# One more weight buffer, the last norm's weights loaded last, a rearranged last norm, and half of the first gather as bf16 products

## The chip, the cores and the metric

One NeuronCore of a Trainium2 chip runs the whole program in one launch. It has TensorE (PE in the rows; its weight loads are PEld), VectorE (DVE), ScalarE (ACT), GpSimd (POOL) and a queue engine, SyncE (SP), all in order within themselves and tied by semaphores, and 16 DMA engines. The metric is the device time of one execution in microseconds (us), the median of several. Lower is better.

## The reference

A decoder block on 256 tokens of width 1024 with 16 meta tokens ahead: a mixer, then a mixture of 16 experts, then a last norm. The change touches what follows the mixer.

```python
h = h + concat(y_ssd, y_sc) @ w_out          # 272 x 2048 @ 2048 x 1024
u2 = rmsnorm(h, norm_ffn)
# hier_moe(u2): best of 4 groups, in it the best 2 of 4 experts, weights by softmax
for e in range(16):
    out += combine[:, e:e+1] * ((silu(t @ w_gate[e]) * (t @ w_up[e])) @ w_down[e])   # 1024 x 512, 512 x 1024
h = h + out
return rmsnorm(h, norm_final)[:, 16:]
```

The experts' weights are 96 MB in float32 (16 experts, three matrices of 2 MB), and each is read once.

## The kernel before

**Stages.** First the mixer (about 223 us), then the routing (to about 240 us): tokens stand on partitions in two halves b = 0, 1 of 128, `hh[:, b]` holds their normalised rows, `scores` and `places` mark each token's two experts, `ranks` gives each token its place `rk` in its experts' queues. Then the experts, 64 slots each, in seven units: `UNITS = 6 * [2] + [4]`. The six experts of the first three units are fixed; `sort_experts` sorts the other ten by load and writes `order` (the numbers that the later loads' addresses come from) and `mosti` (whether an expert has more than 64 tokens; a branch at the very end uses it).

**A unit.** `pick` makes a 0/1 matrix P (token to slot), a gather multiplies hh by it on PE, `rows` scales it into X, then `gu` (gate, then up), ACT's Silu and DVE's product `hb`, its transposes `hbp`, then `yd` (down), `weighed` splits the result into two float32r parts, `scatter` adds them into the PSUM tiles `acc[b][n]` (half b of the tokens, half n of the 1024 columns) during the next unit's gate. The next unit's gather stands between a unit's up and down. Unit 0's gather (`gather`, L903) multiplies float32; later ones (`gather3`, L1115) multiply three bf16 parts of hh, whose sum is hh. These parts are made once, after unit 0's X: for each half two ACT copies and two DVE subtractions, and at the end two ACT copies more (L1101 to L1108).

**The stream of weights.** SP issues all weight loads in the order of use, 1 MB each, into `RING + RING2` = 22 + 3 slots, one of which holds hh then. A load waits on SP until its slot's last reader is done: `used(n)` stands after every second quarter of a product. So 24 MB lie ready before unit 0, and its first gate products free the next slots. The last unit's second halves of `w_down` come in pieces (512 KB, then twice 256 KB for each of four experts). `fin`, the last norm's weights repeated on 128 partitions, is a tile of its own of 4 KB a partition, loaded during the mixer (L774).

**The end.** The last unit's down product comes in column thirds of 512, 256 and 256 (`THIRDS`). `squares_of` (ACT) sums squares of acc; `last_norm` takes the root, and per half of tokens DVE multiplies both column halves by root and `fin`, and ACT's queue issues the four stores.

**Order.** It is written out by hand (`manual_schedule`): each engine runs its instructions in the order of the code.

Of the kernel before, what the change touches and what calls it, by code (L numbers as in the profile page):

```python
# [17 lines left out]
KT = 8  # L18
NE, CAP = 16, 64
EPS = 1e-6  # L20
RING, RING2 = 22, 3
# [18 lines left out]
def body(ctx, tc, x, meta_tokens, norm_mix, w_in, ssd_conv_w, ssd_conv_b, dt_bias, A_log, D_skip,  # L40
# [90 lines left out]
    comb = cp.tile([128, 2, NX], F32, name="comb")  # L131
    count16 = cp.tile([128, NE], F32, name="count16")
    chain = cp.tile([128, NE - FIXED, NE - FIXED], F32, name="chain")
    place = cp.tile([128, NE - FIXED], F32, name="place")
    order = cp.tile([128, NE - FIXED], I32, name="order")

    fin = cp.tile([128, D], F32, name="fin")
    lg = cp.tile([128, 2, 20], F32, name="lg")
    cnt = cp.tile([128, 2, 5, 4], F32, name="cnt")
# [600 lines left out]
    for i, (name, j, c, t0) in enumerate(units):  # L740
# [108 lines left out]
    def ranks(b):  # L849

        p = rp[:, 64 + 16 * b:80 + 16 * b]
        T.matmul(p, sup, mem[:, b], start=True, stop=(b == 0))
        if b:
            T.matmul(p, onesb, mem[:, 0], start=False, stop=True)
        V.scalar_tensor_tensor(rk[:, b, 0:NE], mem[:, b], -1024.0, p, op0=OP.mult, op1=OP.add)
# [20 lines left out]
    def sort_experts(counts):  # L876
        m, key = NE - FIXED, place
        t = small("srt", 2 * m * m)
# [21 lines left out]
    def gather(b, q, p, i0=0, i1=4):  # L900

        for i in range(i0, i1):
            T.matmul(p[:, i], hh[:, b].rearrange("p (m k) -> p k m", k=KT)[:, 4 * q + i],  # L903
                     P[:, b], start=(b == 0 and i == 0), stop=(b == 1),
                     skip_group_check=True)
# [57 lines left out]
    P = bp.tile([128, 2, 128], F32, name="P")  # L963
# [33 lines left out]
    def weights(tm):  # L997
# [20 lines left out]
        in_order(comb[:, :, NE:NX], comb[:, :, FIXED:NE], sorting)  # L1018
# [7 lines left out]
    sorting = wk.tile([128, 2 * (NE - FIXED) ** 2], F32, name="sorting", tag="Yl")  # L1026
# [4 lines left out]
    def back(P, cm):  # L1031
# [8 lines left out]
        PT = wk.tile([128, S], F32R, name="PT", tag="PT")  # L1040
# [44 lines left out]
    h3 = wk.tile([128, 2, D], BF, name="h3")  # L1085
    tm = wk.tile([128, S], F32, name="tm", tag="PT")
    X = wk.tile([128, KT, 128], F32, name="X")
    for q in range(2):
        rows(X, xp[q], q)
    weights(tm)  # L1090
    ws0 = wk.tile([128, 1], F32, name="ws", tag="ws")
    P = wk.tile([128, 2, 128], BF, name="P", bufs=2)
    for b in range(2):
        pick(P, 0, b)


    hb0, hb1 = (hh[:, b].bitcast(BF).rearrange("p (j d) -> p j d", j=2) for b in range(2))
    hparts = [[h3[:, 0], hb0[:, 0]], [h3[:, 1], hb0[:, 1]], [hb1[:, 0], hb1[:, 1]]]
    rem = [wk.tile([128, 512], F32R, name="rem", tag=t).bitcast(BF) for t in ("Yh", "Yl")]
    for b in range(2):  # L1100
        A.activation(hparts[0][b], hh[:, b], AF.Copy)  # L1101
        if b == 0:
            A.activation(ws0, eps, AF.Silu)
        V.tensor_tensor(hh[:, b], hh[:, b], hparts[0][b], op=OP.subtract)
        A.activation(hparts[1][b], hh[:, b], AF.Copy)
        V.tensor_tensor(rem[b], hh[:, b], hparts[1][b], op=OP.subtract)
    for b in range(2):
        A.activation(hparts[2][b], rem[b], AF.Copy)  # L1108
# [20 lines left out]
    def over():  # L1129
# [46 lines left out]
    rv = nc.values_load(mosti[0:1], min_val=0, max_val=2 * S)  # L1176
    chosen += nc.values_load_multi_w_load_instructions(
        order[0:1], engines=[mybir.EngineType.SP], min_val=FIXED, max_val=NE - 1,
# [135 lines left out]
```

## Time and profile before

| | us |
|---|---|
| median of 3 runs | 444.64 (443.95 to 445.56) |
| the profiled execution | 445.38 |
| its span, first to last instruction | 443.4 |

| engine | busy us | share of the span |
|---|---|---|
| PE | 423.8 | 96% |
| PEld | 295.0 | 67% |
| DVE | 220.3 | 50% |
| ACT | 159.0 | 36% |
| POOL | 89.1 | 20% |
| DMA, queue of SP | 138.22 MB | 82.5% of 16 engines |

PE's 96% counts pipelined products whose ends are modelled, so it says that PE is seldom idle, not that it is at its peak. The rows are read by stage: where the chain of waits passes, and what the DMA engines do meanwhile.

### The profile page before, as it was taken

To read this page: it belongs to the slowest core of one execution; us is meant where nothing else is said; L and a number is where in the kernel's file an instruction comes from. 1 tells how busy PE (TensorE), PEld (TensorE's weight loads), DVE (VectorE), ACT (ScalarE), POOL (GpSimd) and SP (SyncE) were. 2 spreads that over 40 slices of the span, in tenths; PEclk is the share of its full clock that TensorE was granted. 3 is DMA by queue.
4 is the path that set the end of the run, shared out by engine and by line. 5 is a ranking of instruction groups with operands and counts; after the bars stand their busy time and mean duration, and the time that the engine had idled before them with its cause. 6 is when DMAs were issued, how large, how long until landed. Compare 5 with 4: busy or idle time off the path is not lost.

```text
span 443.4 us, 7446 instructions
## 1 busy us (share of the span) xinstructions
PE 423.8 (96%) x2923; PEld 295.0 (67%) x2923; DVE 220.3 (50%) x465; ACT 159.0 (36%) x247; POOL 89.1 (20%) x113
## 2 busy tenths in 40 slices
PE   8899999899999899999999999999999999999982
PEld 5799999799998899888877363533535335353241
DVE  7769888758795768695557521110212102121013
ACT  6766346645757344744472401010010100101121
POOL 2345334854668154000000000000000000000000
PEclk9999999999999999999999989999999999999997
DMA  8997977066699566599692999999999999999952
GB/s 232 342 312 250 348 250 266 32 191 188 194 360 413 182 209 233 199 407 419 199 362 102 370 400 375 425 418 424 419 421 421 422 418 420 421 418 422 412 224 98
DMA packets 48892, 139.85 MB, mean 315 GB/s; under 512 B 6342, under 2 KB 32342, under 8 KB 36822
## 3 DMA queue, kind: packets, MB, share of 16 engines
q1 hardware_dynamic: 47990, 138.22, 82.5%
q10 hardware_dynamic: 864, 1.12, 0.7%
q8 instruction: 25, 0.41, 0.4%
q14 instruction: 13, 0.11, 0.1%
HBM read 138.26 MB, written 1.06 MB: 314 GB/s over the span
## 4 chain that ended last, share of the span: by engine, by line
PE 64%; DVE 7%; ACT 3%; issue 2%; POOL 1%; DVEq 0%; ACTq 0%
PE gu L1050 22%; PE yd L1050 11%; PE acc L347 10%; PE xp L1115 4%; PE p_c L339 3%; PE acc L1071 3%; PE p_h L339 3%; PE p_b L339 3%; ACT f L310 1%; PE hbp L1057 1%; DVE h L619 1%; PE xp L903 1%; DVE f L326 1%; POOL f L324 1%; DVE h L548 1%
## 5 line engine op out<-in xcount | busy, mean ns | idle before, releaser
L1050 PE MATMUL gu<-w,X 128*64 128x512 f32 (+1 forms) x512 | 100.0, 595 | 0.4 <-DVE X L1082 0.4
L324 POOL TENSOR_TENSOR f<-w,f 128x256 fp32r<-128x256 f32 x96 | 82.6, 892 | 87.5 <-ACT f L310 77.7
L310 ACT ACTIVATE f<-w 128x1024 fp32r<-128x1024 f32 x64 | 67.1, 1054 | 35.9 <-POOL f L324 12.6
L1050 PEld LDWEIGHTS gu<-w,X 128*64 128x64 f32 (+1 forms) x512 | 31.3, 130 | 61.2 <-issue 59.5
L326 DVE TENSOR_TENSOR f<-w,f 128x1024 fp32r<-128x1024 f32 x40 | 50.6, 1264 | 17.4 <-ACT f L310 17.4
L1050 PE MATMUL yd<-w,hd 128*64 128x512 f32 (+2 forms) x288 | 50.9, 548 | 0.5 <-DVE hd L1060 0.5
L347 PE MATMUL acc<-f,h 128*128 128x512 f32 x192 | 44.8, 391 | 0.0
L1202 DVE TENSOR_TENSOR hb<-hb,gu 128x512 f32<-128x512 f32 x7 | 4.8, 688 | 74.0 <-PE gu L1050 71.9
L347 PEld LDWEIGHTS acc<-f,h 128*128 128x128 f32 x192 | 35.5, 188 | 7.7 <-issue 0.4
L1065 ACT ACTIVATE Yh<-yd,ws 128x512 fp32r<-128x512 f32 x13 | 8.9, 688 | 79.2 <-PE yd L1050 62.5
L1050 PEld LDWEIGHTS yd<-w,hd 128*64 128x64 f32 (+1 forms) x288 | 16.7, 128 | 29.3 <-issue 25.5
L1066 DVE SCALAR_TENSOR_TENSOR Yl<-yd,ws,Yh 128x512 fp32r<-128x512 f32 x12 | 9.0, 751 | 53.6 <-PE yd L1050 38.5
L1115 PE MATMUL xp<-P,hh 128*128 128x128 bf16 x192 | 20.1, 232 | 0.0
L1115 PEld LDWEIGHTS <-hh 128*128 128x128 bf16 x192 | 18.8, 149 | 1.6 <-issue 1.6
L1115 PE MATMUL xp<-P,h 128*128 128x128 bf16 x96 | 17.7, 235 | 1.6 <-ACT hb L1196 1.6
L339 PE MATMUL p_z<-uh,f 128*128 128x256 f32 x128 | 17.3, 285 | 1.9 <-POOL f L324 1.9
L339 PE MATMUL p_c<-uh,f 128*128 128x258 f32 x128 | 16.8, 283 | 1.3 <-DVE h L607 1.3
L339 PE MATMUL p_xs<-uh,f 128*128 128x272 f32 x128 | 18.0, 292 | 0.0
L1196 ACT ACTIVATE hb<-gu 128x512 f32<-128x512 f32 x7 | 4.2, 594 | 37.0 <-PE gu L1050 37.0
L339 PEld LDWEIGHTS p_z<-uh,f 128*128 128x128 f32 x128 | 15.6, 188 | 2.4 <-POOL f L324 2.3
L339 PE MATMUL p_b<-uh,f 128*128 128x256 f32 x128 | 16.6, 281 | 0.7 <-DVE h L607 0.7
L1042 ACT ACTIVATE PT<-ptp 128x256 fp32r<-128x256 f32 x7 | 2.7, 385 | 39.7 <-PE ptp L1038 39.7
(331 smaller groups left out, 648.5 us busy)
## 6 DMA issues: line engine op xcount, KB each, us to landing
w<-in_expert_w_gate SPq DMA_DIRECT2D x32, 1024.0 KB, 11.7
w<-in_expert_w_up SPq DMA_DIRECT2D x32, 1024.0 KB, 14.5
w<-in_expert_w_down SPq DMA_DIRECT2D x28, 1024.0 KB, 13.6
w<-in_w_in SPq DMA_DIRECT2D x23, 1024.0 KB, 7.2
w<-in_w_out SPq DMA_DIRECT2D x8, 1024.0 KB, 9.4
abc<-adr SPq DMA_DIRECT2D x2, 1024.0 KB
w<-in_expert_w_down SPq DMA_DIRECT2D x4, 512.0 KB
w<-in_expert_w_down SPq DMA_DIRECT2D x8, 256.0 KB, 10.5
```

The source lines that it names most:

```text
L310: A.activation(h, src, AF.Copy)
L324: G.tensor_tensor(l[:, k:k + 2], src[:, k:k + 2], h[:, k:k + 2].bitcast(F32), op=OP.subtract)
L326: V.tensor_tensor(l, src, h.bitcast(F32), op=OP.subtract)
L339: T.matmul(p, st_[:, k, :], mv[:, k, t0:], start=(k == 0 and st_ is terms[0][0] and mv is uh), stop=(k == KT - 1 and mv is ul))
L347: T.matmul(acc[b][n], st_[:, 128 * b:128 * (b + 1)], mv[:, 512 * n:512 * (n + 1)], start=False, stop=False, skip_group_check=True)
L548: V.tensor_tensor(yt(4 * hf, 4), yt(4 * hf, 4), v["zs"][:, 4 * hf:4 * hf + 4], op=OP.mult)
L1050: T.matmul(o[c * s:c * s + c], X[:, 128 * k + c * s:128 * k + c * s + c], ws_, start=first_, stop=last_, tile_position=(0, c * s))
L1065: A.activation(Yh, y, AF.Copy, scale=ws)
L1066: V.scalar_tensor_tensor(Yl, y, ws, Yh.bitcast(F32), op0=OP.mult, op1=OP.subtract)
L1071: T.matmul(acc[b][n], PT[:, 128 * b:128 * (b + 1)], part, start=False, stop=stop and part is Y[-1], skip_group_check=True)
L1115: T.matmul(p[:, i], hparts[j][b].rearrange("p (m k) -> p k m", k=KT)[:, 4 * q + i], P[:, b], start=(j == b == 0), stop=(j == 2 and b == 1))
L1202: V.tensor_mul(hb, hb, g)
```

## The change

- **Buffer.** `fin` leaves its early tile. The small routing tiles (`chain`, `place`, `count16`, `comb`, `lg`, `cnt`) become views of one tile `early`, which later is `PT`. The room makes a 26th slot, `RING3 = 1`, in memory that the routing's work tiles held; it opens, with one load, after the routing.
- **Loads.** `fin` is loaded into a freed slot in the last unit, behind the last piece of weights. SP reads `order` after unit 0's up, and all engines read `mosti` after unit 1's down; before, both came ahead of unit 0's gate.
- **Gather of unit 0.** Half b = 0 stays float32. Half b = 1 is split into its three bf16 parts at once and gathered by 24 bf16 products; half b = 0 is split after X.
- **Sorting.** `sort_experts` runs after X and after that split, ahead of `weights`.
- **Last norm.** acc times `fin` for the first column half goes into `wh` before the root is known; ACT then scales it, DVE does the second column half only; the stores are issued by SP and ACT, two each. The second third's result is split into float32r parts (`Y1`), the last third is `Y2`.

```diff
-RING, RING2 = 22, 3
+RING, RING2, RING3 = 22, 3, 1
@@ in the mixer
             load(RING2, right)
-            nc.sync.dma_start(fin, raw(norm_final, 0, [[0, 128], [1, D]]))
@@ routing
-    gather(0, 0, xp[0])
+    gather(0, 0, xp[0], 0, 3)
     for i in range(4):
         places(1, i)
-    gather(0, 1, xp[1], 0, 1)
     ranks(1)
-    gather(0, 1, xp[1], 1, 4)
-    pick(P, 0, 1)
+    P1 = bp.tile([128, 2, 128], BF, name="P1")
+    A.activation(h3[:, 0], hh[:, 1], AF.Copy)
+    V.tensor_tensor(hh[:, 1], hh[:, 1], h3[:, 0], op=OP.subtract)
+    A.activation(h3[:, 1], hh[:, 1], AF.Copy)
+    V.scalar_tensor_tensor(rk[:, 1, 0:NE], mem[:, 1], -1024.0, rp[:, 80:96], op0=OP.mult, op1=OP.add)
+    pick(P1, 0, 1)
+    rem1 = hh[:, 1].bitcast(BF)[:, 0:D]
+    V.tensor_tensor(rem1, hh[:, 1], h3[:, 1], op=OP.subtract)
+    gather(0, 0, xp[0], 3, 4)
+    gather(0, 1, xp[1])
...
-    sort_experts(rp[:, 96:112])
-    for q in range(2):
-        gather(1, q, xp[q])
+    for js in ((0, 1), (2,)):
+        for k in range(KT):
+            for j in js:
+                T.matmul(xp[k // 4][:, k % 4], (h3[:, 0], h3[:, 1], rem1)[j]..., P1[:, 1], start=False, ...)
     es.close()
+    ring3 = ctx.enter_context(tc.tile_pool(name="ring3", bufs=RING3, side="right"))
+    load(RING3, ring3)
@@ after unit 0's X
+    A.activation(hparts[0][0], hh[:, 0], AF.Copy)
+    V.tensor_tensor(hh[:, 0], hh[:, 0], hparts[0][0], op=OP.subtract)
+    A.activation(rem, hh[:, 0], AF.Copy)
+    V.tensor_tensor(hparts[2][0], hh[:, 0], rem, op=OP.subtract)
+    A.activation(hparts[1][0], rem, AF.Copy)
+    sort_experts(rp[:, 96:112], sorting[:, 0:2 * (NE - FIXED) ** 2])
     weights(tm)
@@ the end
+    def by_weights(b, n):
+        V.tensor_tensor(wh[:, b], acc[b][0], fin[:, 0:512], op=OP.mult)
...
             for b in range(2):
                 squares_of(b, 0)
+                by_weights(b, 0)
+                first_sum(b)
         else:
-            V.tensor_scalar(Y1[:, 256:512], y, ws, None, op0=OP.mult)
+            V.tensor_scalar(Y2, y, ws, None, op0=OP.mult)
```

**VectorE from the last expert mark of the routing to the first steps after X** (mem marks the experts, rk the places, X is unit 0's gathered input). Before, the end of the sort stands ahead of X:

```order
L895 TENSOR_TENSOR place<-place,rp 128x10
L896 TENSOR_REDUCE most<-rp 128x1
L897 TENSOR_REDUCE srt<-place 128x1
L898 TENSOR_TENSOR mosti<-most,srt 128x1
L1082 TENSOR_TENSOR X<-xp,gf 128x512 x2
L1003 TENSOR_REDUCE tm<-lg 128x10
```

and in the changed kernel (h_79 is h3, the bf16 parts):

```order
L855 SCALAR_TENSOR_TENSOR mem<-early 128x16
L984 TENSOR_TENSOR hh<-hh,h_79 128x1024
L986 SCALAR_TENSOR_TENSOR rk<-mem,rp 128x16
L875 TENSOR_TENSOR P_2676<-sl,rk 128x128
L989 TENSOR_TENSOR hh<-hh,h_79 128x1024
L1102 TENSOR_TENSOR X<-xp,gf 128x512 x2
L1114 TENSOR_TENSOR hh<-hh 128x1024
L1116 TENSOR_TENSOR hh<-hh,rem 128x1024
L889 SCALAR_TENSOR_TENSOR early<-rp,early 128x10
```

The sort moved behind X and behind two subtractions of half 0; two subtractions of half 1 moved ahead of X.

**SP at the end of the routing**, before (w_2606 is the 24th of the experts' loads, w_2814 the first into a slot that unit 0 frees):

```order
L113 DMA w_2604<-in_expert_w_down 128x2048
L113 DMA w_2606<-in_expert_w_down 128x2048
L1176 TENSOR_LOAD mosti
L1176 ISA x2
L1177 TENSOR_LOAD order
L113 DMA w_2814<-in_expert_w_gate 128x2048
```

and in the changed kernel (w_2722 is the load into the new slot, w_2790 the first into a freed one):

```order
L113 DMA w_2598<-in_expert_w_down 128x2048
L113 DMA w_2600<-in_expert_w_down 128x2048
L113 DMA w_2722<-in_expert_w_gate 128x2048
L113 DMA w_2790<-in_expert_w_gate 128x2048
L113 DMA w_2792<-in_expert_w_gate 128x2048
```

The reads of mosti and order are gone from here, and one load more stands there; it waits for the last expert counts of the routing (DVE), a routing product (PE) and an ACT copy.

**VectorE at the end**, before:

```order
L1066 SCALAR_TENSOR_TENSOR Y<-yd,ws,Yh 128x512
L1258 TENSOR_SCALAR Y_3920<-yd,ws 128x256
L1266 TENSOR_SCALAR s_2804<-s_2804 128x1 x2
L1278 RECIPROCAL s_2803<-s_2803 128x1
L1281 SCALAR_TENSOR_TENSOR o<-acc_68,s_2803,fin 128x512
L1281 SCALAR_TENSOR_TENSOR o<-acc_69,s_2803,fin 128x512
```

and in the changed kernel (oh holds wh and Y2):

```order
L1086 SCALAR_TENSOR_TENSOR Y_3932<-yd,ws,Y_3932 128x256
L1266 TENSOR_TENSOR oh<-acc_68,fin 128x512
L1269 TENSOR_SCALAR s_2780<-s_2780 128x1
L1266 TENSOR_TENSOR oh<-acc_70,fin 128x512
L1269 TENSOR_SCALAR s_2780<-s_2780 128x1
L1295 TENSOR_SCALAR oh<-yd,ws 128x256
L1310 RECIPROCAL s_2779<-s_2779 128x1
```

Two products with fin now stand ahead of the last third's weighing (L1258 before, L1295 now).

## Rows read from the trace of the kernel before

**Rows 1.** The chain that ended last, unit 0 and part of unit 1: start us, us, what.
```profile
239.80 13.95 PE gu L1050 x64
254.21 1.04 ACT hh L1108
260.84 7.02 PE yd L1050 x32
284.14 0.22 PE ptp L1035 x2
284.52 1.64 PE xp L1115 x24
288.18 7.02 PE yd L1050 x32
```

**Rows 2.** Timeline of routing and unit 0's start: start us, us, engine, line, form.
```profile
228.77 2.34 ACT L813 ACTIVATE hh<-hh,rsh 128x1024 f32<-128x1024 f32 x2
235.34 4.07 PE L903 MATMUL xp<-P,hh 128*128 128x128 f32 x16
235.52 0.17 DVE L880 SCALAR_TENSOR_TENSOR place<-rp,count 128x10 f32<-128x10 f32 x1 [1.07 <-PE rp L980]
238.90 0.16 DVE L898 TENSOR_TENSOR mosti<-most,srt 128x1 int32<-128x1 f32 x1
240.18 0.18 DVE L1003 TENSOR_REDUCE tm<-lg 128x10 f32<-128x40 f32 x1
240.77 1.04 ACT L1101 ACTIVATE h<-hh 128x1024 bf16<-128x1024 f32 x1
244.54 0.49 DVE L865 TENSOR_TENSOR P<-sl,rk 128x128 bf16<-128x128 f32 x2
247.29 1.23 DVE L1106 TENSOR_TENSOR rem<-hh,h 128x1024 bf16<-128x1024 f32 x1 [1.12 <-ACT h L1105]
```

**Rows 3.** Stretches of the stream: us, busy of engines, clock share, DMA share, GB/s.
```profile
235.40:244.30 8.90, 8.51 (x41) 5.77 (x40) 7.78 (x36) 2.67 (x4) 0.00 (x0) 1.00 0.02 6
265.00:267.00 2.00, 2.00 (x12) 0.72 (x10) 0.00 (x0) 0.00 (x0) 0.00 (x0) 1.00 0.76 205
267.00:273.00 6.00, 6.00 (x27) 2.20 (x23) 1.90 (x4) 1.37 (x2) 0.00 (x0) 1.00 0.99 359
273.00:426.00 153.00, 151.55 (x966) 63.75 (x968) 24.79 (x46) 14.26 (x24) 0.00 (x0) 1.00 1.01 419
```

**Rows 4.** The chain in the last unit: its gate and up, thirds 1 and 2, third 3.
```profile
410.46 10.53 PE gu L1050 x96
423.37 6.42 PE yd L1050 x63
430.91 1.86 PE yd L1050 x32
```

**Rows 5.** The page's group of DVE's product of PSUM by SBUF (mean ns of one).
```profile
L1202 DVE TENSOR_TENSOR hb<-hb,gu 128x512 f32<-128x512 f32 x7 | 4.8, 688 | 74.0 <-PE gu L1050 71.9
```

**Rows 6.** Timeline of the end: a sum of squares, the last third's weighing, second and last store.
```profile
431.78 0.20 ACT L1240 ACTIVATION_READ_ACCUMULATOR o<-acc 128x1 f32 x1
432.85 0.48 DVE L1258 TENSOR_SCALAR Y<-yd,ws 128x256 f32<-128x256 f32 x1 [3.73 <-PE yd L1050]
436.81 0.34 ACTq L1282 DMA_DIRECT2D out<-o  x1
438.32 1.15 ACTq L1282 DMA_DIRECT2D out<-o  x1
```

**Rows 7.** Loads by line: KB, us from issue to landing; this one was issued at 184.4.
```profile
fin<-in_norm_final SPq DMA_DIRECT2D x1, 512.0 KB, 12.0
```

**Rows 8.** The tile mosti: its read into PE's registers (ns, start us).
```profile
L1176 PEldq TENSOR_LOAD <-mosti x1: 492/492/492, 239.1 to 239.1; - x1
```

**Rows 9.** Stretches by clock: columns as in rows 3.
```profile
255.80:259.60 3.80, 3.80 (x36) 3.75 (x36) 2.00 (x4) 0.21 (x1) 0.00 (x0) 0.57 1.01 420
421.00:421.83 0.83, 0.00 (x0) 0.00 (x0) 0.69 (x1) 0.00 (x0) 0.00 (x0) 1.00 1.01 395
```

More of the change, by code (lines that the diff above doesn't have):

```diff
@@ L130, in body, with part_of @@
     rk = cp.tile([128, 2, NX], F32, name="rk")
[L131 to L134, printed above, removed]
+    m = NE - FIXED
+    early = cp.tile([128, 2 * NX + 206], F32, name="early", tag="PT")
+    at_ = [0]
+    def part_of(n):
+        at_[0] += n
+        return early[:, at_[0] - n:at_[0]]
+    chain = part_of(m * m).rearrange("p (i j) -> p i j", i=m)
+    place = part_of(m)
+    count16 = part_of(NE)
+    comb = part_of(2 * NX).rearrange("p (b e) -> p b e", b=2)
+    lg = part_of(40).rearrange("p (b i) -> p b i", b=2)
+    cnt = part_of(40).rearrange("p (b s i) -> p b s i", b=2, i=4)
     order = cp.tile([128, NE - FIXED], I32, name="order")
-    fin = cp.tile([128, D], F32, name="fin")
-    lg = cp.tile([128, 2, 20], F32, name="lg")
-    cnt = cp.tile([128, 2, 5, 4], F32, name="cnt")
+    h3 = cp.tile([128, 2, D], BF, name="h3")
     selg = cp.tile([128, 2, 4], F32, name="selg")
@@ L874, in in_order, with sort_experts @@
         V.tensor_reduce(out_, t, axis=AX.X, op=OP.add)
-    def sort_experts(counts):
+    def sort_experts(counts, t):
         m, key = NE - FIXED, place
-        t = small("srt", 2 * m * m)
         c = counts[:, FIXED:NE]
@@ L962, in body @@
     busy(1)
-    P = bp.tile([128, 2, 128], F32, name="P")
+    P = bp.tile([128, 1, 128], F32, name="P")
     pick(P, 0, 0)
@@ L1094, in body @@
         pick(P, 0, b)
[L1097 to L1108, printed above, removed]
     def gather3(P, X, q):
@@ L1174, in over @@
                         scatter(b, n, PTo, Yo)
-    rv = nc.values_load(mosti[0:1], min_val=0, max_val=2 * S)
-    chosen += nc.values_load_multi_w_load_instructions(
-        order[0:1], engines=[mybir.EngineType.SP], min_val=FIXED, max_val=NE - 1,
-        skip_runtime_bounds_check_because="a sum of one of the numbers FIXED to NE - 1 and of zeros")[1]
     left = {}
@@ L1196, in body @@
                 A.activation(hb, g, AF.Silu)
-                if not last:
+                if last:
+                    fin = slot("fin", free.pop(0))[:, 0:D]
+                    nc.sync.dma_start(fin, raw(norm_final, 0, [[0, 128], [1, D]]))
+                else:
                     Pn = wk.tile([128, 2, 128], BF, name="P", bufs=2)
@@ L1206, in body @@
             hd = turned(hb)
+        if u == 0:
+            chosen += nc.values_load_multi_w_load_instructions(
+                order[0:1], engines=[mybir.EngineType.SP], min_val=FIXED, max_val=NE - 1,
+                skip_runtime_bounds_check_because="a sum of one of the numbers FIXED to NE - 1 and of zeros")[1]
         PT, ws = back(P, cparts[:, :, places_of(u)])
@@ L1228, in rest @@
             return weighed(y, ws)
+        if u == 1:
+            rv = nc.values_load(mosti[0:1], min_val=0, max_val=2 * S)
         keep = []
@@ L1232, in body, with first_sum, root @@
         left[0, 3] = [lambda b=b, PT=PT, k=keep: scatter(b, 1, PT, k[0]) for b in range(2)]
+    oh = slot("oh", free.pop(0))
+    wh, Y2 = oh[:, 0:1024].rearrange("p (b d) -> p b d", b=2), oh[:, 1024:1280]
     oo = slot("o", free.pop(0)).rearrange("p (b d) -> p b d", b=2)
-    Y1 = wk.tile([128, 512], F32, name="Y1", tag="X")
+    Y1 = wk.tile([128, 2, 256], F32R, name="Y1", tag="X")
     Y = [wk.tile([128, 512], F32R, name="Yh", tag="Yh"), slot("Y", free.pop(0)).bitcast(F32R)[:, 0:512]]
+    def by_weights(b, n):
+        V.tensor_tensor(wh[:, b], acc[b][0], fin[:, 0:512], op=OP.mult)
+    def first_sum(b):
+        V.tensor_scalar(s4[:, b, 0:1], s4[:, b, 0:1], 1.0 / D, EPS, op0=OP.mult, op1=OP.add)
+    def root(b):
+        A.activation(s3[:, b:b + 1], s4[:, b, 1:2], AF.Sqrt, bias=s4[:, b, 0:1], scale=1.0 / D)
     def squares_of(b, n):
@@ L1278, in last_norm @@
             V.reciprocal(s3[:, b:b + 1], s3[:, b:b + 1])
[L1279 to L1282 removed]
+            V.scalar_tensor_tensor(oo[:, b, 512:1024], acc[b][1], s3[:, b:b + 1], fin[:, 512:1024], op0=OP.mult,
+                                   op1=OP.mult)
+            nc.sync.dma_start(raw(out, b * 128 * D + 512, [[D, 128], [1, 512]]), oo[:, b, 512:1024])
+        for b in range(2):
+            A.activation(oo[:, b, 0:512], wh[:, b], AF.Copy, scale=s3[:, b:b + 1])
+            A.dma_start(raw(out, b * 128 * D, [[D, 128], [1, 512]]), oo[:, b, 0:512])
     last_norm()
```

42 lines of the change are left out of this document (21 added, 21 removed).

## The prediction, made before the changed kernel was run

> **What bounds the kernel now.** I read the chain of waits first, then the stretches of the stream, then the timelines where the two meet. From unit 0 on the chain is PE almost alone. From unit 0's down product to unit 1's it takes 288.18 - 260.84 = 27.34 us [rows 1], and the later units repeat that. Beside it the stream of weights runs at 419 GB/s with all DMA engines busy from 273 to 426 us [rows 3]. A unit needs 12 loads of 1.05 MB; at 419 GB/s a load takes 2.5 us, so a unit's loads take 30 us, longer than PE's 27.3. PE lives on the 24 loads that lie ready, and that lead is used up in the last unit: its first two thirds of the down product take 6.42 us, while 96 products of the same size took 10.53, that is 0.11 each, so that the first third (32 of them) is worth 3.51 and the second, by the third of the same width, 1.86 [rows 4]. 6.42 - 3.51 - 1.86 = 1.05 us is waiting for weights. So PE and the stream end level, and only what moves both moves the end. Where both can gain is early: the DMA engines stand still from 235.4 to 244.3 us, since all slots are full until unit 0's gate frees the first, and they fall to 205 and 359 GB/s between 265 and 273 [rows 3]. And unit 0 itself is slow: from its gate's start plus 13.95 (253.75) to its down product it needs 7.09 us, where unit 1 needs 288.18 - 284.14 = 4.04 [rows 1].
>
> **Part 1: the start of unit 0's gate.** Today the sort on DVE runs from 235.52 to 239.06, the float32 gather of half 1 on PE from 235.34 to 239.41 [rows 2], and X begins only behind the sort; the gate starts at 239.80 [rows 1], 0.74 us after the sort's end. In the changed kernel the products ahead of that gather are the same ones in another order, so PE is again free for half 1 at 235.34. Its 24 bf16 products have the shape of those of unit 1, which take 1.64 us [rows 1]: end at 236.98 instead of 239.41. Their parts must be ready: ACT ends its two scalings at 228.77 + 2.34 = 231.11, a copy takes 1.04, a subtraction 1.23 [rows 2], and copy, subtraction, copy, subtraction with 0.05 for each handover end at 235.8. The last third of the products, which alone needs that, begins at 235.34 + 1.09 = 236.4; 0.6 us of cover. X then starts at 237.0 and the gate 0.8 later, at 237.8 to 237.9: **1.9 us earlier**. Bounds: 1.5 (the split 0.5 beyond its cover) to 2.1.
>
> **Part 2: inside unit 0.** The chain waits at 254.21 for an ACT copy (the last of the bf16 parts) [rows 1], behind it PE's clock falls: 0.57 granted from 255.8 to 259.6 [rows 9]. Now the parts come before the sort. DVE after X: 237.0 + 2 x 0.65 = 238.3, subtraction, ACT's copy, subtraction to 241.9, the sort's 3.54 to 245.4, then weights, their parts and two picks, which today go from 240.18 to 245.03 (4.85) [rows 2], to 250.3, and the next unit's two picks (0.49) to 250.8. PE's up product ends at 237.9 + 13.95 = 251.85. So the wait goes, and unit 0 falls to the 4.04 of unit 1: **3.05 us**. The work that hides this is unit 0's gate and up; the cover is 1.0 us. If it is gone, up to the whole 3.05 is lost.
>
> **Part 3: the stream.** The new slot's load waits for routing steps of about 232 us, and the DMA engines have the earlier loads to do until 235.4; its 2.5 us fill a part of the idle stretch [rows 3]. The first freed slots come 1.9 earlier. The dip at 265 to 273 cost 2 x (1 - 205/419) + 6 x (1 - 359/419) = 1.0 + 0.9 us; it stands where the eight loads freed by the gate and up are through (244.3 + 8 x 2.5 = 264.3) and unit 0's late down product has freed no others. With that product 4.95 us earlier its slots come at about 259.5 and the eight are through at 262.4, so the dip goes, or at least its first part. The stream's end moves by 1.9 + 2.5 + 1.0 to 1.9 = 5.4 to 6.3 us. PE's own work moves by 1.9 + 3.05, and by 1.05 more if no weight is late: 6.0. The later of the two counts: **5.8 us** (5.3 to 6.0) at the end of the second third. The old load of `fin`, issued at 184.4 [rows 7], lay among loads that were all through when the stream came to rest at 235.4 [rows 3], so its going gains nothing.
>
> **Part 4: the end.** Two products of PSUM by `fin`, 0.69 each like the product of hb [rows 5], now stand on DVE ahead of the last third's weighing (`Y2`), behind which PE's last products and the root wait. They can start behind ACT's sums of squares, the second of which ends at 431.98 [rows 6]; with the small sums DVE is through at 433.15, and the weighing that started at 432.85 [rows 6] starts 0.3 later (0 to 0.45). Against it DVE has two products behind the root instead of four, ACT takes two scalings, and two queues issue the stores. I put the last store's issue at 438.0 instead of 438.32, the 0.3 included; that issue lasted 1.15 us where an earlier one lasted 0.34 [rows 6], and with two stores on a queue the 0.8 may go or stay. End: **0.5 us less** (+0.1 to -1.1).
>
> `fin` comes behind the last piece of weights: 0.5 MB, 1.25 us at 419 GB/s. It is wanted by DVE's first product with it, when ACT's first sum is done, some 0.6 us ahead of the second's 431.98 [rows 6]; that is 1.6 us behind the end of the second third, 423.37 + 6.42 = 429.79 [rows 4], and about 2 us behind the use of the last piece. Taken at nothing; above, the row of its old load gives 12.0 us from issue to landing [rows 7], with full loads ahead of it in the queue, so I leave it 0.7 in the range.
>
> `mosti` is read into the registers of all engines between units 1 and 2 instead of ahead of unit 0. On PE that takes 0.49 us from 239.1 [rows 8], and PE's products of the gather went on until 239.41 beside it [rows 2], so with products queued it is hidden: nothing, at most 0.5. SP's reads stand where its next load waits for a slot anyway. With small exposures of this kind I add 0.2.
>
> [...]
>
> Sum: -5.8 - 0.5 + 0.2 = **-6.1 us**. The profiled execution took 445.38 us (443.4 of span and 2.0 around it), so 439.3; it lay 0.74 above the median of the three runs, and against the median the forecast is 444.64 - 6.1 = **438.5**.
>
> **The rivals.**
>
> *The clock falls at unit 0's gate.* PE will stand for 0.85 us between gather and gate, with short bf16 products ahead of it. [...] Against it: the gap of 0.83 us at 421.0 left it at 1.00 [rows 9]. Price: 3.8 x 0.43 = 1.6 us on both PE and the freed slots: 440.1. [...]
>
> *DVE's cover in unit 0 is gone.* The eight us of sort and weights now lie behind four 1024-wide passes. If they end 2 us later than I sum, PE waits again and its clock falls again; at worst the 3.05 are lost: 441.5. Against it: every duration is one that the trace shows on the same shapes.
>
> *The new slot doesn't do what it says.* Its load goes out only with the first freed slots, because a work tile that lay there is held until the gather's end. Then the stream gains only 1.9 + 1.0, or 3.8 at best, and PE waits 2 to 3 us more in the last unit: about 441.
>
> *Slower: `fin` arrives late.* DVE stands at its first product with `fin`, and behind it stand `Y2`, PE's last products, the root and all stores. It decides from 2 us after the last piece on, and each us more is a us of the end. To be slower than before by what can be told it must be 7.4 us late; the 12.0 of its old load [rows 7] would make it some 5 us late, 443.5. For slower a broadcast of one 4 KB row would have to be slower still; its old load shows a dip, but no such thing.
>
> **How the numbers follow.** Forecast 438.5, chance 0.75, its own range 437.3 to 439.8 from the bounds (start 0.4, stream 0.5, end 0.6, reads and fin 0.7). Clock 0.09 (440.1). Cover 0.05 (441.5). Slot 0.06 (441). Late fin or another stall that turns it slower 0.03; 0.02 that they cancel to no change. The range holds the forecast, the clock and part of the slot's case: 437.0 to 441.0. A measurement of this kernel tells about 0.3% (1.3 us) from no change: faster 0.95, same 0.02, slower 0.03.
>
> **What would show it.** Right: gate of unit 0 starting at about 237.9; one load landing in the idle stretch at about 238; no wait between unit 0's up and down and a clock of 1.00 there; a unit 1 that starts 5 us earlier; full DMA from about 243 without a dip; at most 0.5 us of waiting for weights in the last unit; `Y2` 0.3 us later after the third than before, the last store about 0.3 us earlier relative to it. Wrong: a gate at 238.5 or later, a clock below 1.00 in unit 0, PE waiting for P or for hh's parts at its end, weights late in the last unit by over a us, or DVE waiting for a DMA ahead of its first product with `fin`.

## The result, and the profile after

| | changed kernel | kernel before |
|---|---|---|
| first comparison, median (runs) | 440.49 us (4; 439.99 to 441.85) | 445.10 us (4; 443.95 to 446.78) |
| second comparison, another chip job | 440.9 us (5; 440.26 to 442.2) | 446.33 us (17; 444.05 to 447.29) |

The ratio was 0.9892 in the first comparison (95% interval 0.9863 to 0.9921) and 0.9887 in the second (0.9864 to 0.9910). The forecast was 438.5 with a range of 437.0 to 441.0. The time is in that range, though not in the 437.3 to 439.8 that the forecast gave as its own; the sign is right, and of the 6.1 us forecast 4.6 came in the first comparison and 5.4 in the second.

The first profile of the changed kernel (span 439.8) can't be laid beside the rows of before as it stands. In the middle of the mixer, far ahead of any edit, TensorE's clock had fallen. The stretches of that profile (us, busy of PE, PEld, DVE, ACT, POOL, granted clock, DMA share, GB/s):

```profile
86.00:89.00 3.00, 1.75 (x12) 1.52 (x14) 0.61 (x1) 1.06 (x1) 1.83 (x2) 0.87 0.00 0
89.00:92.00 3.00, 3.00 (x25) 2.21 (x25) 0.00 (x0) 1.33 (x2) 2.16 (x4) 0.56 0.52 129
```

and of a second profile of the same kernel (run e1_again below, span 438.2):

```profile
86.00:89.00 3.00, 1.72 (x14) 1.51 (x16) 0.64 (x1) 1.30 (x2) 1.83 (x2) 1.00 0.00 0
89.00:92.00 3.00, 3.00 (x38) 2.75 (x35) 1.53 (x6) 1.09 (x2) 2.21 (x4) 1.00 0.62 165
```

In 89 to 92 us the first did 25 products at a granted clock of 0.56, the second 38 at 1.00. Behind that the first is about 1.6 us late for good. So I read the changed kernel from the second profile. Its chain of waits from the routing to unit 1 (start us, us, what):

```profile
231.91 1.67 PE xp L912 x6
...
236.13 1.55 PE xp L1002 x24
...
237.71 0.70 DVE X L1102
...
238.46 13.95 PE gu L1070 x64
...
252.79 1.61 PE xp L1131 x24
...
256.42 7.02 PE yd L1070 x32
...
283.72 7.02 PE yd L1070 x32
```

and the place of the first gather in the chain of the kernel before:

```profile
231.26 2.62 PE xp L903 x10
```

Its stretches of the stream, which answer to [rows 3]:

```profile
236.00:240.00 4.00, 3.22 (x35) 2.16 (x35) 2.75 (x4) 1.65 (x3) 0.00 (x0) 1.00 0.66 274
240.00:244.40 4.40, 4.40 (x22) 1.44 (x20) 2.98 (x10) 2.11 (x2) 0.00 (x0) 1.00 0.29 60
265.00:267.00 2.00, 2.00 (x10) 1.01 (x10) 0.20 (x1) 0.69 (x1) 0.00 (x0) 1.00 1.02 422
267.00:273.00 6.00, 6.00 (x28) 2.17 (x26) 0.95 (x3) 0.08 (x1) 0.00 (x0) 1.00 1.01 422
```

One load (274 GB/s for 4 us, 1.1 MB) now runs in the stretch that stood idle, and the dip at 265 to 273 is gone. And the last unit, for [rows 4]:

```profile
418.86 5.37 PE yd L1070 x64
424.23 1.13 PE acc L1091 x4
425.36 1.86 PE yd L1070 x32
427.22 0.67 PE acc L1299 x4
```

Stage by stage, with the ends of each stage from these chains and from [rows 1, 4]:

| stage | before | changed | difference | forecast |
|---|---|---|---|---|
| start to the first gather | 231.26 | 231.91 | +0.65 | 0 |
| first gather to unit 0's gate | 8.54 | 6.55 | -1.99 | -1.9 |
| gate to unit 0's down product | 21.04 | 17.96 | -3.08 | -3.05 |
| unit 0's down to the last unit's down | 162.53 | 162.44 | -0.09 | 0 |
| last unit, two thirds of the down product | 6.42 | 5.37 | -1.05 | -0.85 |
| last scatter of these and third three | 2.99 | 2.99 | 0 | 0 |
| end of third three to the end of the span | 10.62 | 10.98 | +0.36 | -0.5 |
| span | 443.4 | 438.2 | -5.2 | -6.1 with 0.2 of reserve |

The two ends of the table are what the forecast missed; between them it was right to 0.4 us. The first row is nothing that the change can be held to: in the eight profiles of this study without a fall of the clock in the mixer, whose code up to there is the same but for the old load of `fin` and the place of some tiles, the first gather starts anywhere from 231.15 to 232.80. The last row is the question that the experiments had to answer. It is itself one execution's: seven profiles hold the changed kernel's last norm with the branch behind it (this one, the first one, e2, e4, e7, e8 and e10), and in them the same stretch takes from 10.6 to 11.3 us, where the one profile of the kernel before has 10.62.

### The profile page after: what moved, and what is told of

It reads as the page before. It is cut to its first block, busy times and chain, and to the rows that moved or that the text cites. A ratio compares the mean times of both kernels' runs of the same rounds, so it can differ in the third digit from the quotient of the medians.

```text
span 439.8 us, 7474 instructions
## 1 busy us (share of the span) xinstructions
PE 420.5 (96%) x2931; PEld 291.2 (66%) x2931; DVE 221.1 (50%) x466; ACT 159.5 (36%) x248; POOL 89.0 (20%) x113
## 4 chain that ended last, share of the span: by engine, by line
PE 65%; DVE 5%; ACT 2%; issue 1%; DMA 1%; POOL 1%; ACTq 0%; DVEq 0%
PE gu L1070 22%; PE yd L1070 11%; PE acc L357 10%; PE xp L1131 4%; PE p_c L349 3%; PE p_h L349 3%; PE acc L1091 3%; PE p_b L349 3%; DMA w<-in_w_out 1%; PE xp L912 1%; ACT f L320 1%; PE hbp L1077 1%; DVE f L336 1%; DVE h L629 1%; POOL f L334 1%
## 5 line engine op out<-in xcount | busy, mean ns | idle before, releaser
L1070 PEld LDWEIGHTS gu<-w,X 128*64 128x64 f32 (+1 forms) x512 | 30.4, 130 | 62.4 <-issue 60.3
L1070 PE MATMUL yd<-w,hd 128*64 128x512 f32 (+2 forms) x288 | 49.8, 547 | 0.5 <-DVE hd L1080 0.5
L349 PE MATMUL p_h<-uh,f 128*128 128x258 f32 x128 | 17.0, 285 | 0.0
```

The source lines that it names most:

```text
L349: T.matmul(p, st_[:, k, :], mv[:, k, t0:], start=(k == 0 and st_ is terms[0][0] and mv is uh), stop=(k == KT - 1 and mv is ul))
L1070: T.matmul(o[c * s:c * s + c], X[:, 128 * k + c * s:128 * k + c * s + c], ws_, start=first_, stop=last_, tile_position=(0, c * s))
```

## The experiments

Each kernel is compared with the kernel before, timed on the same chip in the same job; the kernel before stood at 446.3 (17 runs, e1 to e4), 446.5 (16, e5 to e8), 446.25 (11, e9 to e11) and 445.65 (7, e12).

**e1_again: the changed kernel once more.**

> The changed kernel once more, as the yardstick of the other runs of this chip. In its first profile TensorE's granted clock stood at 0.55 to 0.59 from 88 to 92 us, in the middle of the mixer, far ahead of any edit, and everything behind it came about 2 us later than in the kernel before. Theory (accident of that execution): here the stretch has a granted clock of 1.00 and the first gather stands where it stands before the change, within 0.5 us; time 440.0 to 440.6, 4.5 us less than the kernel before. Rival (the change brings it, by the missing load of fin or by other addresses): the same fall of the clock at 88 us, span about 439.8.

Median 440.9. The clock stayed at 1.00, so the fall of the first profile was an accident of that execution. Of the fourteen profiles of this study six have such a fall at this place (0.50 to 0.88 granted on the mean from 89 to 92 us; one of them is of the kernel before without its branch) and eight have none (1.00); all fourteen have a wait of PE for GpSimd of 1.9 us ahead of it. The rival falls.

**e2_noslot: without the extra buffer.**

```diff
-    ring3 = ctx.enter_context(tc.tile_pool(name="ring3", bufs=RING3, side="right"))
-    load(RING3, ring3)
```

> The changed kernel without the extra buffer: its load goes to a slot that unit 0 frees. Theory (PE and the stream end level, the load fills idle DMA time and is worth its 2.5 us): the stream still gains 1.9 us from the earlier gate and 1.0 to 1.9 from the dip, PE 5.05, so PE waits for weights again in the last units, and the time is 1.5 to 3.2 us above the changed kernel. Rival (the stream has slack, the end is PE's alone): within 0.4 us of the changed kernel.

Median 442.62, 1.7 us above the changed kernel. A stretch of the stream, the chain in the last unit, and the wait list of PE's weight loads from 400 to 430 us (what waited, for what: us in total, times, longest):

```profile
236.00:240.00 4.00, 3.22 (x28) 1.72 (x28) 2.42 (x3) 1.44 (x3) 0.00 (x0) 1.00 0.02 4
```

```profile
418.28 7.13 PE yd L1068 x60
...
425.41 0.62 PE yd L1068 x2
```

```profile
PEld yd L1068 <- DMA w<-in_expert_w_down: 2.7, 6, 0.6
```

The DMA engines stand still again from 236 to 240 us, and the two thirds take 7.13 + 0.62 = 7.75 us instead of 5.37: 2.38 us of waiting for weights, about the duration of one load (2.5). The buffer is worth about its load; the rival (slack in the stream) falls.

**e3_oldtail: the old last norm in the changed kernel.**

```diff
-            weighed(y, ws, [Y1[:, 0], Y1[:, 1]])
+            A.activation(Y1[:, 0:256], y, AF.Copy, scale=ws)
...
-            V.scalar_tensor_tensor(oo[:, b, 512:1024], acc[b][1], s3[:, b:b + 1], fin[:, 512:1024], ...)
-            nc.sync.dma_start(raw(out, b * 128 * D + 512, ...), oo[:, b, 512:1024])
+            for n in range(2):
+                V.scalar_tensor_tensor(oo[:, b, c], acc[b][n], s3[:, b:b + 1], fin[:, c], ...)
+                A.dma_start(raw(out, b * 128 * D + 512 * n, ...), oo[:, b, c])
```

> The changed kernel with the last norm of the kernel before: DVE scales all four quarters behind the root, ACT issues all four stores, the last third is weighed ahead of the last products in one float32 step; fin still lies in a freed slot. Theory from the profile (the new last norm issues its last store 0.5 us earlier, but the stores' data end no earlier, the stretch behind the last third is 0.4 us longer): 0.4 us faster than the changed kernel (0 to 0.8). The prediction's part 4: 0.5 us slower. Rival (the tail of the stores differs from one execution to the next): within 0.3 us.

My theory was wrong. The stretch behind the last third was 438.3 - 426.92 = 11.38 us, 0.40 longer than with the new last norm in e1_again, not shorter. The median of 442.0 lies among runs from 439.29 to 442.54 and doesn't separate anything of that size: the two fastest have a mean granted clock of 0.995, the other four 0.989 to 0.992. So the new last norm is not what lengthened the end against the kernel before: the old one, in the same place, is no shorter. That the end differs between executions, as the rival says, the seven profiles named above bear out (10.6 to 11.3 us with the same code at the end); the rival's 0.3 us these medians can't test. Something that both have in common, outside the last norm's own code, had to be looked for, and the stores' queue showed it (e5, below).

**e4_sortfirst: the sort ahead of X again.**

```diff
+    sort_experts(rp[:, 96:112], sorting[:, 0:2 * (NE - FIXED) ** 2])
     for q in range(2):
         rows(X, xp[q], q)
...
-    sort_experts(rp[:, 96:112], sorting[:, 0:2 * (NE - FIXED) ** 2])
     weights(tm)
```

> The changed kernel with the sort of the experts put back ahead of X on DVE; the bf16 gather of half 1, the extra buffer and all else stay. Theory (X waits for DVE, not for PE): the sort's 3.5 us start when the split of half 1 is through, X comes 2.3 us later, unit 0's gate and with it the first freed slots as well, so the whole rest and the end: 2.3 us slower than the changed kernel (1.8 to 2.6). Rival (the bf16 gather alone gave the earlier gate, the sort's place is free): within 0.5 us.

Median 443.56, 2.7 us above the changed kernel, a little over the range. The first gather starts at 231.95 in this profile, the gate 8.65 us later instead of 6.55: 2.1 us by DVE, as expected, and no earlier than before the change (8.54). But the gate itself took 15.65 us instead of 13.95. The timeline's row of its first products (start us, us, engine, line, form, idle before and what ended it) and the stretches around it:

```profile
240.60 1.12 PE L1070 MATMUL gu<-w,X 128*64 128x512 f32 x2 [2.90 <-DVE X L1102]
```

```profile
238.00:240.00 2.00, 0.00 (x0) 0.00 (x0) 1.79 (x11) 0.00 (x0) 0.00 (x0) 1.00 0.32 135
240.00:242.00 2.00, 1.40 (x4) 0.54 (x6) 2.00 (x3) 0.00 (x0) 0.00 (x0) 0.66 0.03 8
242.00:244.00 2.00, 2.00 (x6) 0.49 (x4) 0.82 (x2) 1.06 (x1) 0.00 (x0) 0.50 0.00 0
244.00:246.00 2.00, 2.00 (x12) 0.72 (x10) 1.15 (x6) 1.21 (x3) 0.00 (x0) 0.99 0.00 0
```

PE stood for 2.90 us, and then the granted clock was 0.50 from 242 to 244 us: 6 products in these two us, where the next two have 12 at 0.99. That is the first rival of the prediction, on the gate that it named, with a price of 1.70 us where it put 1.6. It did not happen in the changed kernel, where PE stands for 0.78 us there and the clock stays at 1.00. From the first gather to the end of third three this profile takes 199.12 us, 3.81 more than e1_again, while the medians differ by 2.7; whether all twelve runs had the fall isn't known.

**e5_noif and e6_before_noif: both kernels without the branch at the end.** The branch skips a pass for experts with more than 64 tokens; these data have none, and the pass is left out.

```diff
-    with tc.If(rv > CAP):
-        over()
-        ...
-        last_norm()
```

> The changed kernel without the branch at its end (the pass for experts with more than 64 tokens, which these data don't enter, is left out). In the traces so far one 16 KB instruction load lies among the four stores in every kernel, and the last store packets follow one another singly, 80 ns apart, as on one DMA engine that is late: where that load took 1.0 us (before) the last packet ended 4.36 us after the first had started, where it took 1.6 us (changed, and with the old last norm) 4.7 to 5.1. Theory (the load for the jump over the pass holds up one DMA engine's share of the stores, that is why the end got no shorter): without the branch the packets end 3.2 to 3.7 us after the first starts, and the stretch from the end of the last third's products to the end of the span shrinks from 10.98 to 9.5 to 10.0 us. Rival (the stores' own queues are late): 10.7 to 11.1 us, the load or no load.

> The kernel before, also without the branch at its end and without the pass behind it. Theory: here the load cost less (1.0 us), so the stretch from the last third's products to the end of the span shrinks less than in the changed kernel, from 10.62 to 10.0 to 10.3 us, and the difference between the two kernels without the branch is the forecast's 6.1 us (5.7 to 6.7) where it was 5.2 between the undisturbed profiles. Rival: the difference stays 5.2. It also gives a second profile of the mixer of the kernel before: the first gather within 0.5 us of 231.26.

Medians 438.22 and 443.2: 2.7 and 3.3 us below the same kernels with the branch. The DMA view of e1_again from 431 to 437 us (GB/s in 40 equal slices; the queue of instruction loads: packets, MB, share; the stores: count, KB each, us from issue to landing):

```profile
GB/s 0 0 0 259 382 328 410 396 410 410 369 328 328 355 355 382 341 342 410 341 341 232 41 82 68 68 55 14 27 27 27 27 27 27 0 0 0 0 0 0
...
q8 instruction: 1, 0.02, 1.6%
...
out<-o ACTq DMA_DIRECT2D x2, 256.0 KB, 4.3
out<-o SPq DMA_DIRECT2D x1, 256.0 KB, 4.4
```

and of e5_noif, the same six microseconds:

```profile
GB/s 0 0 0 0 0 0 0 96 355 341 382 423 355 369 382 423 382 314 396 437 382 342 382 423 382 341 82 0 0 0 0 0 0 0 0 0 0 0 0 0
...
out<-o SPq DMA_DIRECT2D x2, 256.0 KB, 2.3
out<-o ACTq DMA_DIRECT2D x2, 256.0 KB, 2.3
```

and of the kernel before, 437 to 442 us:

```profile
GB/s 311 360 410 344 410 328 393 377 492 360 295 99 279 377 360 328 410 197 33 16 33 33 66 147 328 410 360 426 344 148 16 33 33 16 16 0 0 0 0 0
...
q8 instruction: 1, 0.02, 1.3%
...
out<-o ACTq DMA_DIRECT2D x3, 256.0 KB, 3.5
```

Without the branch the stores run through and stop at once. With it they end in a tail of 27 GB/s, about a sixteenth of the stream's 419 [rows 3]. I read that as one of 16 DMA engines, still at its share of the last stores because a 16 KB instruction load lay in its way. That it is one engine's share is inferred from the rate and from the packets, which follow singly at 80 ns; the trace doesn't number the engines. In the kernel before the stores also fall to 16 to 66 GB/s between 439.25 and 439.9, behind the long issue of the last one (1.15 us from 438.32 on). By the packets of the stores:

| kernel | third three's end to the first packet | first to last packet | last packet to the end of the span | 16 KB load among them |
|---|---|---|---|---|
| before | 4.23 | 4.36 | 2.0 | 1.01 us |
| changed (e1_again) | 4.27 | 4.68 | 2.0 | 1.56 us |
| changed, first profile | 4.27 | 4.76 | 2.0 | 1.68 us |
| changed, fin's old load (e7) | 4.27 | 4.69 | 2.3 | 1.57 us |
| changed, no buffer (e2) | 4.27 | 4.37 | 2.0 | 1.18 us |
| changed, sort first (e4) | 4.27 | 4.36 | 2.0 | 0.96 us |
| changed, two banks (e10) | 4.27 | 4.36 | 2.0 | 0.96 us |
| changed, halves (e8) | 4.27 | 4.58 | 2.0 | 0.96 us, 0.9 us later than in e4 and e10 |
| changed, old norm (e3) | 4.23 | 5.13 | 2.0 | 1.62 us |
| changed, no branch (e5) | 4.27 | 2.88 | 1.4 | none |
| before, no branch (e6) | 4.24 | 3.02 | 1.4 | none |
| changed, old norm, no branch (e12) | 4.24 | 3.01 | 1.4 | none |

So the branch costs the end 2.0 us in the kernel before, and 2.4 in e1_again (2.0 to 2.7 over the seven profiles). Another 0.2 to 0.3 lies outside the span: time less span is 2.1 us in e1_again and 1.8 in e5. Among the kernels with the new last norm the tail goes with the length of that one load: where it took 0.96 to 1.18 us and came as in e1_again the packets end 4.36 us behind the first, as in the kernel before; where it took 1.56 to 1.68 they end 4.7 to 4.8 behind. The theory of e5 holds in kind; the gain is larger than I wrote (the stretch is 8.60 us, not 9.5 to 10.0; the packets end 2.88 us behind the first, 0.3 below my bound, and 0.6 us more went behind the last one). e6 came out otherwise than I wrote in all three points. The stretch is 8.66 us, not 10.0 to 10.3: the branch costs the kernel before almost as much as the changed one. The first gather starts at 232.76, with the clock's fall in the mixer. And the difference between the profiles without the branch is 442.0 - 436.5 = 5.5 us, between my 5.7 and the rival's 5.2. Part of what is missing there is in the last unit, where the kernel before this time took 5.63 us for the two thirds, not 6.42 [rows 4]:

```profile
424.75 5.63 PE yd L1050 x64
```

Its wait for weights is 0.26 in this execution and 1.05 in the other. What the change removes there is not the same each time.

**e12_oldtail_noif: the price of the last norm alone.** The edits of e3 and e5 together; the pass is left out here too.

> The changed kernel with the last norm of the kernel before and without the branch and the pass behind it, so that no instruction load disturbs the stores: it prices part 4 by itself. With the new last norm the stretch from the end of the last third's products to the end of the span was 8.55 us without the branch. Part 4 as predicted (0.5 us gained by the new last norm): 9.0 to 9.1 us here. Rival (the new last norm only moves work about, the stores' packets follow one another either way): 8.5 to 8.7.

Third three's products end and the last ones begin, in e12 and in e5, at

```profile
428.03 1.32 PE acc L1295 x4
...
427.90 0.67 PE acc L1299 x4
```

436.7 - 428.03 = 8.67 us, where the new last norm has 436.5 - 427.90 = 8.60. The rival holds: without instruction loads the new last norm is worth 0.1 us. The table shows why. The first packet starts no earlier (4.24 and 4.27), since the root comes first in both, and from there on 1.05 MB need 2.88 to 3.02 us, 350 to 365 GB/s. When the last store was issued made no difference here, with data queued ahead of it: its issue starts at 433.6 in e12 and 433.0 in e5, 5.6 and 5.1 us behind third three's end.

**e7_finload: the early load of `fin` put back.**

```diff
             load(RING2, right)
+            nc.sync.dma_start(h3.rearrange("p b d -> p (b d)").bitcast(F32), raw(norm_final, 0, [[0, 128], [1, D]]))
```

> The changed kernel with the old early load of the last norm's weights put back at its old place, into a tile that lies idle there; nobody reads it. The prediction holds its going for worth nothing: within 0.3 us of the changed kernel, the first gather where it stands without it. Rival (the load held up the loads of weights behind it): the extra buffer's load and those before it end 1 us later, and the weights come late in the last unit again, up to 1.2 us.

Median 440.79 against 440.9. Two rows of its chain:

```profile
232.03 1.67 PE xp L913 x6
...
418.99 5.37 PE yd L1071 x64
```

From the first gather to the last down product it takes 186.96 us, in e1_again 186.95, and the two thirds take 5.37 in both. Its going gains nothing, as the prediction said.

**e8_halves and e10_halves2: is the end PE's now?** In the last unit PE waits while DVE copies the turned product; both kernels cut that copy in two, for DVE and ACT.

```diff
-        V.tensor_copy(hd, p)
+        V.tensor_copy(hd[:, 0:256], p[:, 0:256])
+        A.activation(hd[:, 256:512], p[:, 256:512], AF.Copy)
```

> The changed kernel, in the last unit alone the copy of the turned product to SBUF cut in two, half on DVE and half on ACT, since PE waits for it there (0.70 us of DVE). Theory (in the changed kernel the end is PE's, the weights lie ready): the last down product starts 0.30 to 0.35 us earlier and the end comes as much earlier, as fast or faster than the changed kernel. Rival (PE and the stream still end level): the start moves, but the first two thirds take as much longer, for weights, and the end stays.

It tested nothing (median 440.69): the program's semaphores let ACT's copy start only after DVE's, so the copies ran one after the other (start us, us, engine, line, form):

```profile
418.69 0.42 DVE L1081 COPY hd<-hbp 128x256 f32<-128x256 f32 x1 [0.84 <-PE hbp L1077]
...
419.15 0.38 ACT L1082 ACTIVATE hd<-hbp 128x256 f32<-128x256 f32 x1 [6.82 <-DVE hd L1081]
```

Both read one PSUM bank and both write one tile `hd`; which of the two ties them isn't shown, since e10 parts both. With two transposes into each of two banks, and each pair copied to a tile of its own:

> [...] Here, in the last unit alone, two transposes go to each of two banks, DVE copies the first pair, ACT the second. The last down product then starts 0.6 to 0.7 us earlier after the up product (1.65 us instead of 2.33). Theory (the end is PE's, the weights lie ready): the first two thirds stay at 5.37 us and the end comes 0.6 us earlier. Rival (PE and the stream end level): the two thirds take as much longer, for weights.

```profile
418.47 0.70 DVE hb L1228
...
420.24 5.56 PE yd L1072 x63
```

The down product starts 1.77 us after DVE's product hb instead of 2.27: 0.50 gained, where I had written 0.6 to 0.7. The two thirds take 5.56 instead of 5.37, and the end of third three lies 194.99 us behind the first gather instead of 195.31. So 0.32 of 0.50 stays; the wait list names no transfer for the other 0.19, so neither the theory nor the rival holds whole, and its cause stays open. The median (440.65) can't tell 0.3 us.

**e9_roll and e11_both: a shorter jump.** The pass behind the branch is written as a loop over its three rounds instead of three copies, so that the jump over it is shorter, to see whether the 16 KB loads go with its length; e11 adds the halves of e10.

```diff
-            for r in range(1, S // CAP):
+            with tc.For_i(1, S // CAP, 1):
```

> The changed kernel with the pass behind the branch written as a loop over its three rounds instead of three copies; it computes the same, and the jump over it on PE is some 70% shorter. Without the branch the stretch from the end of the last third's products to the end of the span was 8.55 us, with it 10.98, with two 16 KB instruction loads. [...] Rival (the branch itself costs, wherever it leads): the loads are gone and the stretch is still above 10 us.

> Both at once: the pass as a loop and the last unit's halves. Theory: the gains add, 2.0 to 3.0 us below the changed kernel, 438 us or a little less, if the shorter jump takes the loads away; 0.6 us below it if not. Rival: no faster than the changed kernel.

Medians 439.1 and 438.49, ratios to the kernel before 0.9839 (0.9812 to 0.9866) and 0.9839 (0.9811 to 0.9867), where the changed kernel's was 0.9887 (0.9864 to 0.9910). The chain of e11_both in the last unit:

```profile
415.83 0.70 DVE hb L1228
...
417.60 5.54 PE yd L1072 x64
...
426.14 0.67 PE acc L1309 x4
```

and its DMA view from 428 to 445 us, without a row of q8 (its slices are longer than above):

```profile
GB/s 0 0 0 0 0 106 381 362 395 361 371 390 97 43 0 0 0 19 0 0 0 0 0 0 0 0 0 0 0 0 0 0 0 0 0 0 0 0 0 0
...
q14 instruction: 3, 0.02, 0.4%
```

The stretch behind third three is 10.3 us in both. The 16 KB load that lay among the stores is gone, and with it only 0.3 to 1.0 us (10.3 against the seven profiles' 10.6 to 11.3), where the kernel without the branch has 8.60; the stretch stays above 10 us, as the rival has it. But the rival isn't shown cleanly: in e9_roll one 16 KB load remains just behind PE's last product (109 GB/s for 0.15 us at 431.2), and the packets end 3.60 us behind the first instead of 4.68. 8 KB loads remain too (three in each kernel from 428 us on), and 2.4 us pass behind the last packet where 1.4 do without the branch. So the branch has a price beside the 16 KB load among the stores, about 1.7 us here; what it consists of I did not try. e11 computes the whole of the reference and is faster than both kernels: 7.8 us below the kernel before, where the changed kernel is 5.4 below. By the profiles the two gains are 0.32 us ahead of the end and 0.3 to 1.0 in it (0.7 against e1_again); the medians show more for the shorter jump alone (439.1 against 440.9, in different jobs), and the runs of either kernel spread over 2 to 3 us, so only the sign is certain.

By the traces two 16 KB loads come within 5 us of PE's last product with the branch (before and e1_again), none comes behind 428 us without it (e5 and e12), and one with the shorter jump (e9). What sets such a load off isn't shown. That stores end later where such loads run is what e5 and the table show: with a 16 KB load among them the packets take 4.36 to 5.13 us, without the branch 2.88 to 3.02.

## Why the prediction was right, and where it was wrong

**What bounds the kernel: right.** PE and the stream did end level, to about a us. The wait of 1.05 us in the last unit (0.26 in e6) went with the change and came back as 2.38 in e2.

**Part 1 (1.9 us): right, 1.99.** X at 237.71 is 5.80 us behind the first gather, the forecast's 237.0 was 5.74. e4 shows that the sort's new place is needed for it: with the bf16 gather alone X waits 2.1 us longer for DVE, and nothing is gained. That the sort's move alone would gain nothing either follows from the float32 gather's end at 239.41 [rows 2]; no run shows it.

**Part 2 (3.05 us): right, 3.08.** DVE is through with the picks at 251.19 and PE's up product ends at 252.41: 1.2 us of cover where 1.0 was forecast, and the clock stays at 1.00, where the kernel before has the fall of [rows 9] and has it again in e6 (0.70 granted from 256 to 260 us). This is read from the chain; no run takes this part back alone.

**Part 3 (5.8 us at the end of the second third): right in its mechanism, a little small.** Counted from the first gather, the end of the second third, and of third three with it, moved by 6.21, just above the 5.3 to 6.0 given; PE's own sum was 6.0. Counted from e6, the other profile of the kernel before, it moved by 5.31, for most of the wait for weights isn't there. The stream had been taken for the later of the two; it was just in time (0.3 us of waiting is left on one weight load). The slot fills the idle stretch and is worth 2.4 us; the old load of `fin` is worth nothing (e7); `fin` itself and the reads of `mosti` cost nothing: from unit 1's down product, in which PE now reads `mosti`, to unit 2's it is 27.32 us in both kernels. The reserve of 0.2 wasn't needed.

**Part 4 (0.5 us): the step that failed, a term mis-sized.** Measured: 0.1 us by e12, where no instruction load disturbs it. The 0.36 us by which the end is longer in e1_again goes with the longer load of that execution; in e2, e4 and e10, where the load took 0.96 to 1.18 us, the end is 10.6 to 10.7 us, as before. Three things in it:
- The delay of `Y2` by 0.3 us did not come. The products by `fin` begin behind ACT's first sum of squares, not behind the second, and DVE is through with both just in time:

```profile
425.88 0.69 DVE L1266 TENSOR_TENSOR oh<-acc,fin 128x512 f32<-128x512 f32 x1 [0.52 <-ACT o L1275]
...
427.29 0.48 DVE L1295 TENSOR_SCALAR oh<-yd,ws 128x256 f32<-128x256 f32 x1
```

  The weighing starts 0.07 us behind third three's end, as before.
- I measured the end by the issue of the last store. That issue did come earlier: it starts 5.07 us behind third three's end, where it started 5.54 behind. But its data was not waiting for its issue but for the data ahead of it: without the branch the end is set by the first store's start and by the rate, and neither changed by much (first packet 4.24 us behind third three in e12 and 4.27 in e5, then 1.05 MB in 3.01 and 2.88 us). That part is 0.1 us (e12), not 0.5.
- The instruction load among the stores took 1.56 us in e1_again, 0.96 to 1.68 in the seven profiles, and 1.01 before. I had seen that the last store's issue lasted 1.15 us where another lasted 0.34 [rows 6], and held it for something that the queue might keep or lose. With the old last norm it belonged to the branch. The tile view's rows of the four stores (ns minimum, median, maximum; first and last start) with the branch, in e3_oldtail,

```profile
L1309 ACTq DMA_DIRECT2D out<-o x4: 339/350/1913, 430.3 to 432.5; - x4
```

  and without it, in e12_oldtail_noif:

```profile
L1309 ACTq DMA_DIRECT2D out<-o x4: 338/338/357, 431.4 to 433.6; - x4
```

  A row of the profile of before that didn't fit was a sign of the missing term. It is not the whole of it: in e1_again no issue of a store lasts over 0.36 us, and the stores end late all the same. Why the load took 1.0 us in some executions and 1.6 in others, I did not find out.

**The rivals.** The clock at the gate did not fall (1.00, behind a wait of 0.78 us), and e4 shows the case with the price that was put on it. The cover held. The slot did what it says; without it the wait in the last unit (2.4) is inside the 2 to 3 given, and the medians differ by 1.7. `fin` was not late.

**The number.** 438.5 was 2.0 us under the first median. Of that, 0.46 is the kernel before itself, whose median there was 445.10 where I had started from 444.64. About 0.4 is part 4 (0.5 forecast, 0.1 in e12). The rest I can't divide by runs; it is of the size by which executions of one kernel differ: 0.65 us up to the first gather between the two profiles laid side by side, 2.2 where the clock fell in the mixer, up to 0.7 in the length of the load at the end, and a wait for weights in the kernel before that was 1.05 us in the execution I summed from and 0.26 in another. One profiled execution carries such terms into a sum, and the range should have held them. That the time lies in the stated range is partly luck: it is 0.7 us above the forecast's own upper end, 439.8, and the range went on to 441.0 for the rivals of the clock and the slot, neither of which came. The lower end, 437.0, stood for gains that no run of the changed kernel showed.

## What to carry to other kernels

Where stores end a kernel, look at the transfer, not at the issue: the start of the first packet, the rate, and every other load on the DMA engines in those microseconds; here a branch that is not entered cost 2.0 to 2.7 us there, and the rearranged arithmetic gained 0.1. A buffer that filled idle DMA time was worth about its load here (2.4 us of 2.5), because PE and the stream ended level. And a duration in the profile that its neighbours don't have (an issue of 1.15 us among those of 0.34) is a question to be answered before it is summed. So is a term seen in one execution only: the same code at the end took 10.6 to 11.3 us.

## What the runs showed of the hardware

- A branch that is not entered, at the end of this kernel, cost 2.0 to 2.7 us of span: with it two 16 KB instruction loads (before and e1_again; one in e9, with the shorter jump) and one to three of 8 KB come within 5 us of PE's last product, and the stores of a queue take 3.3 to 4.3 us at the median from issue to landing (2.9 to 3.3 with the shorter jump) where they take 2.1 to 2.3 without.
- After a wait of 1.9 us on PE in the mixer the granted clock fell in six of fourteen profiles (0.50 to 0.88 on the mean from 89 to 92 us) and stayed at 1.00 in the other eight; after 2.90 us, with nothing on PE, the next two products took 1.12 us and the clock was 0.50 from 242 to 244 us (e4, one profile); after 0.78 to 0.79 us at the same gate it stayed at 1.00 in all eleven profiles that have that gap.
- The start of the first gather, 230 us into the same code, differed by 1.65 us between executions whose clock stood at 1.00 in the mixer (231.15 in e11, 232.80 in e12).
